# A second block's mixer in one fused kernel: where the state space tables are loaded, and in which order the SSM outputs' matmuls run

## The chip, the cores and the metric

The kernel runs on one core of a Trainium2 chip. A time is the device time of one run in microseconds; the time of a kernel is the median of its runs. All of the work is one program: TensorE (PE in the rows, its weight loads PEld) multiplies, VectorE (DVE), ScalarE (ACT) and GpSimd (POOL) do the rest, and SyncE (SP) issues nearly all transfers.

## The reference, cut to what matters

Two blocks on 256 tokens of 1024 channels. The first has four layers of attention and feed-forward; the second one hybrid layer, whose mixer is what is changed here. Half of the mixer is a state space model (SSM) of 32 groups of 16 channels with 64 states each, half is attention in 8 heads (with 256 tokens one block, so plain causal attention).

```python
h = rmsnorm(x, g_pre_mix)
z = jnp.einsum('bsd,de->bse', h, w_in)                  # 1024 -> 4 * 512
u, q, k, v = jnp.split(z, [D_SSM, D_SSM + D_ATTN, D_SSM + 2 * D_ATTN], axis=-1)
y_ssm = s5_mixer(u, ...)       # scan of the states, y = C states + d u, gelu, y * sigmoid(y w_glu + b)
y_attn = moba_attention(q, k, v)
mix = jnp.concatenate([rmsnorm(y_ssm, g_ssm_out), rmsnorm(y_attn, g_attn_out)], axis=-1)
x = x + rmsnorm(jnp.einsum('bse,ed->bsd', mix, w_out), g_post_mix)
```

## The kernel before

Tokens stand in two tiles of 128 (`t`), weights are streamed from memory once. A weight unit is 256 rows by 512 columns, 512 KB, loaded by `wload` into a buffer `raw` (4 buffers), then split into two parts, `hi` by ScalarE (line 158) and `lo` by VectorE (line 159), with 6 buffers each. `mm3` (lines 178 to 180) does three matmuls per row chunk with them. A projection of 512 columns from 1024 channels has 4 units and 48 matmuls. What is not urgent (transposes, the SSM's inflow) is put on the list `waiting`, from which `pump` emits one piece after each unit, and `drain` all.

The order of each engine's instructions is set by the tile framework at build time: an instruction goes when its data and its buffers are there by the framework's own reckoning, and of those that are ready the one that stands first in the program. Buffers belong to pools with a fixed number each: `big` has nine of 8 KB per partition, for the transposed activations (hT, a pair), the feed-forward's transposed products (fT, a pair per block), qkT, and the SSM's tables. Each engine, SyncE's queue too, then runs its list strictly in order.

The SSM works on chunks of 8 tokens. Its tables are computed from the parameters beside earlier layers and put in memory: `wd` (inflow of a chunk to the states), `ed` (decay and turn of the states, for the scan), `kd` (the response within a chunk) and `vd` (read-out of the states). `get_tables` (line 1107) fetches all of them when the mixer's norm is set up, in `mix2` (line 1388), that is before the last products of the feed-forward layer ahead. `kd` is read as overlapping windows (line 1121), two loads of 1 MB, `vd` (line 1122) too.

`mixer2` (line 1125) then runs:
- the projection to u; its rows go by small transfers (`uc`, line 1143) into chunks on partitions, are turned (`uo`, `ut`), and `inflow` (line 1171) multiplies them with `wd`. `states` (lines 1178 to 1199) scans them on VectorE into `xp`, the state before each chunk;
- one call for the projections to q and k, whose transposes go to qkT;
- the SSM outputs: two PSUM banks `yb`, of 32 x 128 tiles. A tile is in one of four quadrants of 32 partitions (`q_`) and at one of four places (`g8`) of the bank. Each takes one matmul of `ut` (128 rows) with a window of `kd`, then two of `xp` (64 rows, of the real and the imaginary part) with `vd`. `Chain` (line 252) keeps the matmuls of a bank in program order. Gelu follows per bank, into `yo`, and eight small transfers bring it back to tokens on partitions (`ys`, line 1230);
- the attention's numerators: scores (line 1244), masked maximum, exponential (line 546), transposes;
- the projection to v, the transposes of `ys`, the gate with w_glu, the weighted sums, the norms, and w_out.

Of the kernel before, what the change touches and what calls it, by code (L numbers as in the profile page):

```python
# [11 lines left out]
ALU = mybir.AluOpType  # L12
# [54 lines left out]
def tile_kernel(ctx, tc, I, out, upto=99):  # L67
# [54 lines left out]
    def load_gains(names):  # L122
        """Gains of the model's width, by channels on partitions."""
# [58 lines left out]
    def proj(xT, specs, consume, tmaj=False, kx=0, tags=(), mid=None):  # L182
        """specs: (w, first column, columns); consume(i, t, psum[:, :n]); mid: what comes after the first loads."""
# [37 lines left out]
    def outacc(acc, fT, lk, w, gk, nk, first, last, consume=None):  # L221
        """acc[t][n] += fT chunks lk.. times w's row chunks gk.. (two halves of 512 columns)."""
# [22 lines left out]
    class Chain:  # L245
        """Keeps the matmuls of one bank in program order, so that its accumulation groups stay apart."""
# [118 lines left out]
    def rope(v, nh, r2, cos, sin, tag):  # L365
        """v [128, nh, 2 * r2] in place; cos, sin [128, 2 * r2] (sin with its signs)."""
# [8 lines left out]
    def to_T2(dst, d0, src, n, t):  # L375
        """As to_T, in two parts."""
# [8 lines left out]
    def scores(o, q, k, rows, qs, ks):  # L385
        """o = q[rows, *qs].T @ k[rows, *ks], of parts."""
# [6 lines left out]
    def to_T(dst, d0, src, n, t, eng):  # L393
        """dst[:, d0 + i, tokens of t] = src[:, 128 i : 128 (i + 1)].T, i < n <= 4."""
# [14 lines left out]
    def layer_a(P, i, j, close, mid=None):  # L409
# [25 lines left out]
        def soft(hb):  # L435
            """p0 - lambda s0 / s1 p1 by heads, transposed."""
# [50 lines left out]
        # lambda  # L487
# [31 lines left out]
    def tr4(blocks, eng, aT=None):  # L519
        """Four blocks of 128 columns, transposed."""  # L520
# [12 lines left out]
    def heads(E, n, k, scale, nmx, so, p, mask=None):  # L533
        """Softmax numerators of n heads of k columns: p[:, a] = exp(scale * (E - max)), sums to so[:, a]."""
# [13 lines left out]
    def layer_b(P, i, j, close):  # L548
# [75 lines left out]
        def soft(hb):  # L624
            """Probabilities by heads, transposed."""
# [17 lines left out]
        def av(hb, oT):  # L643
            """The heads' outputs, with channels on partitions."""
# [28 lines left out]
    def layer_c(P, i, j, close):  # L673
# [13 lines left out]
        def permuted(g):  # L687
            """The tokens of a dilated group, in order of their phases."""
# [15 lines left out]
        def step(g, hb):  # L704
            """Attention of heads 8 hb .. of group g: a generator, for what is to come between its parts."""
# [25 lines left out]
            for t in range(NT):  # L731
                # keys: a group's own half of the tokens, or the band's columns
                k0 = 128 * t if g else 64 * t
                for e in range(2):
                    for pr in prs:
# [10 lines left out]
                        # statistics by head 8 hb + 2 d + e  # L746
# [34 lines left out]
        def spread(g):  # L781
            """The statistics of a dilated group, back in the order of the tokens."""
# [7 lines left out]
        def dilated(t, hb):  # L790
            """The two dilated groups in one: weighted sums in og[2], statistics in st12."""
# [7 lines left out]
        def total(t, hb, o0):  # L799
            """All groups, over the common sum, transposed."""  # L800
# [43 lines left out]
    def merge(nM, wa, wb, s, sa, sb):  # L844
        """sa, sb [128, 2, n]: (-max, sum) of two key groups; weights exp(max - common max), common sum."""
# [11 lines left out]
    def wsum(o, a, wa, b, wb):  # L857
        """o = a * wa + b * wb, by heads of 64."""
# [9 lines left out]
    class Late:  # L868
        """The vector engine, for work that others go before."""
# [13 lines left out]
    def cmul(ore, oim, ar, ai, br, bi, shape, neg=False):  # L883
        """(ore, oim) = (ar, ai) * (br, bi); neg: oim is the imaginary part's negative, of ai negated."""
# [10 lines left out]
    def ssm_tables():  # L895
        """Pieces of the work, one per step of the generator."""
# [38 lines left out]
        # angle less whole turns, the turn in three parts  # L935
# [14 lines left out]
        # (lambda - 1) / a  # L950
# [20 lines left out]
        # powers of lambda  # L971
# [9 lines left out]
        # b and c  # L981
# [22 lines left out]
        for q_ in range(2):  # L1004
            rs = slice(8 * q_, 8 * q_ + 8)
            # read-out: (re, -im) of c lambda^(i + 1)
# [5 lines left out]
            # impulse response of the first 8 steps  # L1012
# [15 lines left out]
        # the skip, at lag 0  # L1028
# [6 lines left out]
        # by half of the groups, input h, lag (7 of them negative), group of the half as (x, y), output h  # L1035
# [8 lines left out]
        # a chunk's inflow to the states: lambda^j b for the step j before its last, with (j, h) on partitions  # L1044
# [13 lines left out]
        # decay and turn of a chunk of 8 steps, and its powers  # L1058
# [21 lines left out]
    class Prep2(Prep):  # L1080
        """x becomes its rms norm of gain g1; the rest as for Prep of that, with gain g2."""
# [25 lines left out]
    def get_tables():  # L1107
        """The state space model's tables, back on chip."""
        kd, wd, vd, ed = TAB["kd"], TAB["wd"], TAB["vd"], TAB["ed"]
# [330 lines left out]
```

## Time and profile before

| | us |
|---|---|
| runs before | 1806.71, 1807.12, 1802.77 |
| median | 1806.71 |
| span of the profiled execution, first to last instruction | 1804.8 |
| median less that span | 1.9 |
| TensorE busy | 1761.0 |
| DVE busy | 1098.5 |
| ScalarE busy | 923.8 |

Times in the trace count from the first instruction of the profiled execution. A row of a timeline has start, duration, engine, line, operation, output<-inputs, shape and count; equal instructions in a row are merged, and a bracket at the end gives the idle time before and what ended it. The fp32 matmuls of the SSM and of the transposes are two instructions each in the trace; a matmul's duration there runs to its last result, so that the distance of starts, not the duration, is what one costs in a dense stretch.

### The profile page before, as it was taken

To read this page: it belongs to the slowest core of one execution; us is meant where nothing else is said; L and a number is where in the kernel's file an instruction comes from. 1 tells how busy PE (TensorE), PEld (TensorE's weight loads), DVE (VectorE), ACT (ScalarE), POOL (GpSimd) and SP (SyncE) were. 2 spreads that over 40 slices of the span, in tenths; PEclk is the share of its full clock that TensorE was granted. 3 is DMA by queue.
4 is the path that set the end of the run, shared out by engine and by line. 5 is a ranking of instruction groups with operands and counts; after the bars stand their busy time and mean duration, and the time that the engine had idled before them with its cause. 6 is when DMAs were issued, how large, how long until landed. Compare 5 with 4: busy or idle time off the path is not lost.

```text
span 1804.8 us, 24261 instructions
## 1 busy us (share of the span) xinstructions
PE 1761.0 (98%) x9008; PEld 1432.6 (79%) x9008; DVE 1098.5 (61%) x1963; ACT 923.8 (51%) x1497; POOL 71.1 (4%) x100
## 2 busy tenths in 40 slices
PE   8999999999999999999999999999999969999998
PEld 6778888878888877777878888777888857678886
DVE  6766555776554655555676655777976545475554
ACT  6655444675444565655555444674544433554443
POOL 0010000110000000000000000001000000010000
PEclk9999999999999999999999999999999989999999
DMA  7346565524666554555446565534676685346662
GB/s 257 106 124 191 184 190 177 157 94 126 189 187 188 167 141 121 150 154 162 153 118 198 183 190 186 165 117 129 192 245 208 204 211 171 100 134 204 188 187 92
DMA packets 168766, 299.56 MB, mean 166 GB/s; under 512 B 20120, under 2 KB 36464, under 8 KB 167880
## 3 DMA queue, kind: packets, MB, share of 16 engines
q1 hardware_dynamic: 164936, 293.52, 53.5%
q0 software_dynamic: 3712, 4.49, 1.0%
q8 instruction: 71, 1.16, 0.3%
q14 instruction: 47, 0.39, 0.1%
HBM read 288.20 MB, written 8.68 MB: 164 GB/s over the span
## 4 chain that ended last, share of the span: by engine, by line
PE 90%; DVE 3%; DMA 2%; ACT 2%; issue 1%; POOL 1%; SPq 0%; POOLq 0%; DVEq 0%; ACTq 0%
PE psacc L179 13%; PE psacc L180 13%; PE psacc L178 13%; PE psE L178 7%; PE psE L179 6%; PE psE L180 6%; PE psT L178 6%; PE psT L179 6%; PE psT L180 6%; PE psT L280 4%; PE psT L252 3%; PE psE L739 2%; DMA raw<-in_w_in 2%; PE psacc L252 2%; PE psE L280 1%
## 5 line engine op out<-in xcount | busy, mean ns | idle before, releaser
L159 DVE TENSOR_TENSOR lo<-raw,hi 128x1024 fp32r<-128x1024 f32 (+1 forms) x528 | 637.4, 1210 | 482.5 <-ACT hi L158 480.8
L158 ACT ACTIVATE hi<-raw 128x1024 fp32r<-128x1024 f32 (+1 forms) x528 | 552.7, 1048 | 584.5 <-PE psacc L180 239.5
L178 PE MATMUL psacc<-hi,big 128*128 128x512 f32 (+1 forms) x1136 | 456.6, 402 | 1.0 <-ACT big L272 1.0
L180 PE MATMUL psacc<-hi,big 128*128 128x512 f32 (+1 forms) x1136 | 450.1, 396 | 0.0
L179 PE MATMUL psacc<-lo,big 128*128 128x512 f32 (+1 forms) x1136 | 449.4, 396 | 0.0
L180 PEld LDWEIGHTS psacc<-hi,big 128*128 128x128 f32 x1136 | 215.0, 189 | 43.0 <-issue 0.6
L178 PEld LDWEIGHTS psacc<-hi,big 128*128 128x128 f32 x1136 | 214.8, 189 | 42.7 <-issue 2.4
L179 PEld LDWEIGHTS psacc<-lo,big 128*128 128x128 f32 x1136 | 214.7, 189 | 42.3 <-issue 1.6
L178 PE MATMUL psE<-hi,big 128*128 128x512 f32 (+2 forms) x568 | 216.0, 381 | 17.3 <-ACT hi L158 15.6
L180 PE MATMUL psE<-hi,big 128*128 128x512 f32 (+2 forms) x568 | 213.9, 377 | 0.2 <-DVE big L273 0.2
L179 PE MATMUL psE<-lo,big 128*128 128x512 f32 (+2 forms) x568 | 213.9, 377 | 0.0
L178 PE MATMUL psT<-hi,big 128*128 128x512 f32 (+1 forms) x480 | 178.5, 372 | 0.0
L180 PE MATMUL psT<-hi,big 128*128 128x512 f32 (+1 forms) x480 | 178.4, 372 | 0.0
L179 PE MATMUL psT<-lo,big 128*128 128x512 f32 (+1 forms) x480 | 178.3, 372 | 0.0
L178 PEld LDWEIGHTS psE<-hi,big 128*128 128x128 f32 x568 | 108.1, 190 | 38.1 <-ACT hi L158 16.0
L180 PEld LDWEIGHTS psE<-hi,big 128*128 128x128 f32 x568 | 107.9, 190 | 19.4 <-DVE big L273 0.9
L179 PEld LDWEIGHTS psE<-lo,big 128*128 128x128 f32 x568 | 108.2, 190 | 18.3
L178 PEld LDWEIGHTS psT<-hi,big 128*128 128x128 f32 x480 | 90.4, 188 | 15.8 <-issue 0.2
L180 PEld LDWEIGHTS psT<-hi,big 128*128 128x128 f32 x480 | 90.5, 188 | 15.7
L179 PEld LDWEIGHTS psT<-lo,big 128*128 128x128 f32 x480 | 90.5, 188 | 15.6
L546 ACT ACTIVATE p<-psE,st 128x256 f32<-128x256 f32 x96 | 44.5, 471 | 21.9 <-DVE st L544 20.0
L546 ACT ACTIVATE p<-sm,st 128x128 f32<-128x128 f32 (+2 forms) x112 | 45.9, 413 | 18.9 <-DVE st L544 18.8
(292 smaller groups left out, 1639.4 us busy)
## 6 DMA issues: line engine op xcount, KB each, us to landing
raw<-in_f_w_gu SPq DMA_DIRECT2D x176, 512.0 KB, 3.8
raw<-in_f_w_out SPq DMA_DIRECT2D x88, 512.0 KB, 3.5
raw<-in_c_w_qkv SPq DMA_DIRECT2D x72, 512.0 KB, 4.2
raw<-in_a_w_qkv SPq DMA_DIRECT2D x48, 512.0 KB, 4.2
raw<-in_w_gate SPq DMA_DIRECT2D x22, 512.0 KB, 3.7
raw<-in_w_up SPq DMA_DIRECT2D x22, 512.0 KB, 3.6
raw<-in_w_down SPq DMA_DIRECT2D x22, 512.0 KB, 3.5
raw<-in_a_w_o SPq DMA_DIRECT2D x16, 512.0 KB, 3.9
```

The source lines that it names most:

```text
L158: A.activation(hi, raw, AF.Copy)
L159: V.tensor_tensor(lo, raw, hi.bitcast(F32), op=ALU.subtract)
L178: T.matmul(o, a, hi[:, c, :n], start=(first and c == 0), stop=False)
L179: T.matmul(o, a, lo[:, c, :n], start=False, stop=False)
L180: T.matmul(o, b, hi[:, c, :n], start=False, stop=(last and c == nk - 1))
L252: ins = T.matmul(*a, **kw)
L280: T.transpose(pt[:n, i * 128:(i + 1) * 128], src, ident)
L546: A.activation(p[:, a], src[:, a], AF.Exp, bias=nmx[:, a:a + 1], scale=scale, accum_out=so[:, a:a + 1])
L739: T.matmul(E[:, k * a:k * a + k], qkT[64 * e:64 * e + 64, d, cs(t)], qkT[64 * e:64 * e + 64, 4 + d, k0:k0 + k], start=True, stop=True)
```

## The change

`get_tables` is parted in two. `get_inflow` fetches `wd` and `ed` where all tables were fetched; `get_outflow(a)` fetches the half `a` of `kd` and `vd`, and is called after the projection to q (0) and after that to k (1), which become two calls. The numerators' loop is moved ahead of the SSM outputs, with its `drain()`. The SSM outputs of a bank go by kind: first the matmuls of `ut` for all places and quadrants, then those of `xp`, by place, part and quadrant, the quadrant innermost. `start`, which clears the bank's marks in a quadrant, is set only at the first place. Comments and docstrings are dropped.

```diff
-    def get_tables():
+    def get_inflow():
-        kd, wd, vd, ed = TAB["kd"], TAB["wd"], TAB["vd"], TAB["ed"]
+        wd, ed = TAB["wd"], TAB["ed"]
         wt = [big([128, 16, 2, 64]) for _ in range(2)]
-        vt = [big([128, 16, 128]) for _ in range(2)]
-        tt_ = [big([128, 2048]) for _ in range(2)]
         rows = [work([128, 512], "sse") for _ in range(3)]
         for a in range(2):
             nc.sync.dma_start(wt[a], wd[a].rearrange("p (r g q) -> p r g q", r=16, g=2))
         for a, z in enumerate(rows):
             nc.sync.dma_start(z, ed[a])
-        for a in range(2):
-            win = kd[a, :, 0:2048]
-            nc.sync.dma_start(tt_[a], bass.AP(win.tensor, win.offset, [[256, 8], [3840, 16], [1, 2048]]))
-            nc.sync.dma_start(vt[a], vd[a].rearrange("p (r c) -> p r c", r=16))
+    def get_outflow(a):
+        kd, vd = TAB["kd"], TAB["vd"]
+        win = kd[a, :, 0:2048]
+        tt_, vt = big([128, 2048]), big([128, 16, 128])
+        nc.sync.dma_start(tt_, bass.AP(win.tensor, win.offset, [[256, 8], [3840, 16], [1, 2048]]))
+        nc.sync.dma_start(vt, vd[a].rearrange("p (r c) -> p r c", r=16))
+        return tt_, vt
...
-        proj(hT, [(w, 512, 512), (w, 1024, 512)], lambda c, t, p_: consu(1 + c, t, p_))
+        got = []
+        for c in range(2):
+            proj(hT, [(w, 512 + 512 * c, 512)], lambda _, t, p_: consu(1 + c, t, p_))
+            got.append(get_outflow(c))
+        tt_, vt = zip(*got)
...
-        yb = [psum("acc"), psum("acc")]
-        for b in range(2):
-            ym = Chain()
-            for g8 in range(4 * b, 4 * b + 4):
-                for q_ in range(4):
-                    o = yb[b][32 * q_:32 * q_ + 32, 128 * (g8 - 4 * b):128 * (g8 - 4 * b) + 128]
-                    ym(o, utv[:, g8, q_], tt_[g]...[:, pr % 4, pr // 4], start=True, stop=False)
-                    for a in range(2):
-                        ym(o, xp[a][64 * g:64 * g + 64, pr, 0:32], vt[a][64 * g:64 * g + 64, pr], start=False, stop=(a == 1))
...
         drain()
         aTs, sums = {}, {}
...
+        yb = [psum("acc"), psum("acc")]
+        for b in range(2):
+            ym, g8s = Chain(), range(4 * b, 4 * b + 4)
+            at = lambda g8, q_: yb[b][32 * q_:32 * q_ + 32, 128 * (g8 - 4 * b):128 * (g8 - 4 * b) + 128]
+            for g8 in g8s:
+                for q_ in range(4):
+                    ym(at(g8, q_), utv[:, g8, q_], tt_[g]...[:, pr % 4, pr // 4],
+                       start=(g8 == 4 * b), stop=False, skip_group_check=True)
+            for g8 in g8s:
+                for a in range(2):
+                    for q_ in range(4):
+                        ym(at(g8, q_), xp[a][64 * g:64 * g + 64, pr, 0:32], vt[a][64 * g:64 * g + 64, pr], start=False,
+                           stop=(a == 1), skip_group_check=True)
...
         proj(hT, [(w, 1536, 512)], lambda c, t, p_: consu(3, t, p_))
```

## Rows read from the trace of the kernel before

**Rows 1.** The page's first part: busy time, share of the span, instructions

```profile
PE 1761.0 (98%) x9008; PEld 1432.6 (79%) x9008; DVE 1098.5 (61%) x1963; ACT 923.8 (51%) x1497; POOL 71.1 (4%) x100
```

**Rows 2.** The chain of waits in order of time, 1430 to 1620: start, us, what

```profile
1449.62 31.54 DMA raw<-in_w_in
...
1521.36 26.94 PE psacc L252 x184
```

**Rows 3.** Stretches: length, then busy time (count) per engine, clock, DMA share, GB/s

```profile
1437.00:1461.70 24.70, 24.70 (x119) 20.01 (x118) 14.76 (x22) 11.67 (x19) 1.10 (x2) 1.00 0.97 251
...
1466.70:1482.35 15.65, 0.07 (x1) 0.00 (x1) 0.02 (x1) 1.11 (x2) 0.00 (x0) 0.59 0.70 158
1482.35:1486.73 4.38, 4.38 (x11) 3.47 (x11) 3.94 (x7) 3.86 (x8) 1.46 (x1) 0.51 0.57 203
...
1519.02:1548.23 29.21, 29.21 (x200) 15.95 (x199) 8.37 (x10) 4.68 (x7) 0.00 (x0) 1.00 0.34 109
1548.23:1569.40 21.17, 21.17 (x107) 15.07 (x107) 13.81 (x51) 15.97 (x44) 0.00 (x0) 1.00 0.45 119
```

**Rows 4.** TensorE's waits, 1470 to 1610: total us, times, longest

```profile
PE psE L178 <- ACT hi L158: 15.6, 1, 15.6
```

**Rows 5.** SyncE's queue in order of time

```profile
1348.13 2.69 SPq L1056 DMA_DIRECT2D wd<-sswt  x4
...
1437.21 0.37 SPq L155 DMA_DIRECT2D raw<-in_w_in  x1
1437.75 1.29 SPq L1117 DMA_DIRECT2D sse<-ed  x3
...
1440.36 0.97 SPq L1115 DMA_DIRECT2D big<-wd  x2
1441.42 0.69 SPq L1121 DMA_DIRECT2D big<-kd  x1
...
1449.62 38.64 SPq L155 DMA_DIRECT2D raw<-in_w_in  x7
```

**Rows 6.** Stretches of 5 us, columns as in rows 3

```profile
1445.00:1450.00 5.00, 5.00 (x24) 4.14 (x23) 2.64 (x3) 1.70 (x3) 0.00 (x0) 1.00 1.06 383
1450.00:1455.00 5.00, 5.00 (x26) 3.97 (x25) 3.21 (x4) 1.30 (x4) 0.00 (x0) 1.00 1.01 156
```

**Rows 7.** TensorE in order of time, within the SSM outputs

```profile
1523.39 0.41 PE L252 MATMUL psacc<-big,ut 128*32 128x128 f32 x2
1523.73 0.62 PE L252 MATMUL psacc<-big,xp 64*32 64x128 f32 x4
1524.28 0.41 PE L252 MATMUL psacc<-big,ut 128*32 128x128 f32 x2
```

**Rows 8.** TensorE where parts of its array alternate: layers a, b, the tables (line 252)

```profile
45.62 0.29 PE L389 MATMUL psE<-big,big 64*128 64x256 f32 x2
45.74 0.29 PE L390 MATMUL psE<-big,big 64*128 64x256 f32 x2
...
375.18 2.00 PE L252 MATMUL psT<-big,big 128*64 128x256 f32 x16
...
1278.30:1279.81 1.51, 1.51 (x63) 1.51 (x64) 1.00 0.91 283
```

**Rows 9.** From the SSM outputs' end to `ys`: timeline, and transfers' us to landing

```profile
1548.23 0.55 PE L280 MATMUL psT<-con,qs 128*128 128x128 f32 x3
...
1552.41 0.69 DVE L1227 SCALAR_TENSOR_TENSOR yo<-ga,yh 128x512 f32<-128x512 f32 x1
...
1553.24 5.13 SPq L1230 DMA_DIRECT2D ys<-yo  x8
...
ys<-yo SPq DMA_DIRECT2D x8, 64.0 KB, 2.4
```

**Rows 10.** Timeline: the last part of u scaled, the last step of the states

```profile
1491.49 0.69 ACT L1139 ACTIVATE qs<-psE,r 128x512 f32<-128x512 f32 x1 [0.18 <-PE psE L180]
...
1519.22 0.68 DVE L1132 TENSOR_TENSOR xp<-xp,z 128x512 f32<-128x512 f32 x1
```

More of the change, by code (lines that the diff above doesn't have):

```diff
@@ L1117, in get_tables @@
             nc.sync.dma_start(z, ed[a])
-        for a in range(2):
-            win = kd[a, :, 0:2048]
-            nc.sync.dma_start(tt_[a], bass.AP(win.tensor, win.offset, [[256, 8], [3840, 16], [1, 2048]]))
-            nc.sync.dma_start(vt[a], vd[a].rearrange("p (r c) -> p r c", r=16))
-        TAB["got"] = wt, vt, tt_, rows
+        TAB["in"] = wt, rows
+    def get_outflow(a):
[5 more added lines that the diff above has]
+        return tt_, vt
     def mixer2(P, close):
         hT, r = P.hT, P.r
-        wt, vt, tt_, (e_, i_, d_) = TAB["got"]
+        wt, (e_, i_, d_) = TAB["in"]
         w = I["w_in_2"][0]
@@ L1203, in mixer2 @@
         nc.sync.dma_start(caus, I["consts"][:, o_:o_ + w_].rearrange("p (t k) -> p t k", t=NT))
-        proj(hT, [(w, 512, 512), (w, 1024, 512)], lambda c, t, p_: consu(1 + c, t, p_))
-        yb = [psum("acc"), psum("acc")]
-        yo = work([128, 8, 8, 16], "yo")
-        ys = work([128, NT, 512], "ys")
-        for b in range(2):
-            ym = Chain()
-            for g8 in range(4 * b, 4 * b + 4):
-                for q_ in range(4):
-                    g, pr = q_ // 2, (q_ % 2) * 8 + g8
-                    o = yb[b][32 * q_:32 * q_ + 32, 128 * (g8 - 4 * b):128 * (g8 - 4 * b) + 128]
-                    ym(o, utv[:, g8, q_], tt_[g].rearrange("p (i x y h) -> p x y i h", x=4, y=4, h=16)[:, pr % 4, pr // 4],
-                       start=True, stop=False)
-                    for a in range(2):
-                        ym(o, xp[a][64 * g:64 * g + 64, pr, 0:32], vt[a][64 * g:64 * g + 64, pr], start=False, stop=(a == 1))
-            yh = work([128, 8, 64], "yh")
-            A.activation(yh.rearrange("p i (g h) -> p g i h", g=4), yb[b].rearrange("p (g i h) -> p g i h", g=4, i=8), AF.Copy, scale=0.5)
-            ga = work([128, 8, 64], "ga")
-            A.activation(ga, yh, AF.Square, scale=2.0)
-            V.tensor_scalar(ga, ga, 0.044715, 1.0, op0=ALU.mult, op1=ALU.add)
-            tt(ga, ga, yh, ALU.mult)
-            A.activation(ga, ga, AF.Tanh, scale=2.0 * math.sqrt(2.0 / math.pi))
-            V.scalar_tensor_tensor(yo[:, :, 4 * b:4 * b + 4].rearrange("p i g h -> p i (g h)"), ga, 1.0, yh, op0=ALU.add, op1=ALU.mult)
-        for t in range(NT):
-            for q_ in range(4):
-                nc.sync.dma_start(ys[:, t, cs(q_)], yo[32 * q_ + 16 * t:32 * q_ + 16 * t + 16].rearrange("c i g h -> c i (g h)"))
+        got = []
[3 more added lines that the diff above has]
+        tt_, vt = zip(*got)
         drain()
@@ L1249, in mixer2 @@
                     aTs[t, e, pr] = tr4([p_[:, a, cs(c)] for a in range(n) for c in range(t + 1)], (A, V)[e])
+        yb = [psum("acc"), psum("acc")]
+        yo = work([128, 8, 8, 16], "yo")
+        ys = work([128, NT, 512], "ys")
+        for b in range(2):
[3 more added lines that the diff above has]
+                for q_ in range(4):
+                    g, pr = q_ // 2, (q_ % 2) * 8 + g8
+                    ym(at(g8, q_), utv[:, g8, q_], tt_[g].rearrange("p (i x y h) -> p x y i h", x=4, y=4, h=16)[:, pr % 4, pr // 4],
+                       start=(g8 == 4 * b), stop=False, skip_group_check=True)
+            for g8 in g8s:
+                for a in range(2):
+                    for q_ in range(4):
+                        g, pr = q_ // 2, (q_ % 2) * 8 + g8
+                        ym(at(g8, q_), xp[a][64 * g:64 * g + 64, pr, 0:32], vt[a][64 * g:64 * g + 64, pr], start=False,
+                           stop=(a == 1), skip_group_check=True)
+            yh = work([128, 8, 64], "yh")
+            A.activation(yh.rearrange("p i (g h) -> p g i h", g=4), yb[b].rearrange("p (g i h) -> p g i h", g=4, i=8), AF.Copy, scale=0.5)
+            ga = work([128, 8, 64], "ga")
+            A.activation(ga, yh, AF.Square, scale=2.0)
+            V.tensor_scalar(ga, ga, 0.044715, 1.0, op0=ALU.mult, op1=ALU.add)
+            tt(ga, ga, yh, ALU.mult)
+            A.activation(ga, ga, AF.Tanh, scale=2.0 * math.sqrt(2.0 / math.pi))
+            V.scalar_tensor_tensor(yo[:, :, 4 * b:4 * b + 4].rearrange("p i g h -> p i (g h)"), ga, 1.0, yh, op0=ALU.add, op1=ALU.mult)
+        for t in range(NT):
+            for q_ in range(4):
+                nc.sync.dma_start(ys[:, t, cs(q_)], yo[32 * q_ + 16 * t:32 * q_ + 16 * t + 16].rearrange("c i g h -> c i (g h)"))
         proj(hT, [(w, 1536, 512)], lambda c, t, p_: consu(3, t, p_))
@@ L1391, in mix2 @@
         nxt = Prep2(I["final_norm"], gains("final_norm"), gains("g_pre_mix_2"))
-        get_tables()
+        get_inflow()
         return nxt
```

## The prediction, made before the changed kernel was run

> **What bounds the kernel now.** TensorE is busy 98% of the span [rows 1], so a gain has to come out of its idle time or make its work shorter; other engines matter only where TensorE waits for them. I read the chain of waits next, for the second block's mixer. Two pieces of it are long [rows 2]: one load of w_in that is 31.54 us from issue to landing, and 184 instructions of line 252, the SSM outputs, in one run of 26.94 us. The table of stretches gives their weight [rows 3]: after 1466.70 TensorE does nothing for 15.65 us, then runs 11 instructions in 4.38 us at a granted clock of 0.51, the lower of its two levels (1.2 GHz); the SSM outputs fill 29.21 us; from there to 1569.40 the numerators and the v projection take 21.17 us. The list of waits names the idle time: the matmul waits 15.6 us for ScalarE's part `hi` of a weight [rows 4]. SyncE's queue says why [rows 5]: between the second and the third unit of w_in stand `ed`, `wd` and the four loads of `kd` and `vd`, 4 MB that nobody reads before the SSM outputs, and the third unit, issued at 1449.62, lies behind them. The queues stay full, but from 1450 on the rate falls from 383 to 156 GB/s [rows 6]: these tables are slow to read. The first two units, 24 matmuls, keep TensorE busy only to 1466.70.
>
> **Part 1, the loads.** `get_inflow` keeps `wd` and `ed` where they were; `get_outflow(0)` comes after the q projection in the program, `get_outflow(1)` after k. Nothing is added: the same 4 MB in the same four issues. With the third and fourth unit of w_in no longer behind them, they should land before 1461.7, when TensorE comes to them. Removed are the wait, 15.6 us, and the slow clock behind it: 11 instructions at the 0.21 us of the stretch before (24.70 us for 119) are 2.3 us, so 4.38 - 2.3 = 2.1 us. Sum 17.7 us, at most; below nothing this edit alone can't go, since u then has only fewer bytes ahead of it.
>
> What it triggers is the price. The queue's order isn't the program's: the framework sends a load when its buffer is free. The first unit of w_in went ahead of `ed` [rows 5], which the program has earlier. So the tables' place is set by the buffers `big`, nine in all, which I take to be granted in the order of first use: the new hT pair, written just before u's first matmuls, comes before the first `kd` and `vd`, and qkT before the second. The first pair then goes out near 1460. 2.1 MB at 156 GB/s are 13.4 us, to 1473. Queued behind it are the last units of q, the first of k, and the small transfers `uc`, which start the chain to the states; SyncE's queue is in order, and ScalarE, which converts weights in order, holds the scaling of u behind a late unit. u's 48 matmuls last to 1461.8 + 48 x 0.21 = 1472 and two more units lie ready, 5 us, so the cover is just enough. The states end 28 us after u does, as now (the last part of u is scaled at 1491.49, `xp` is done at 1519.9 [rows 10]), so near 1502 to 1506, when k also ends. The second pair can't go before qkT's turn, near 1490, and lands near 1505: the SSM outputs may wait a few us for it. I take 2 us for this part's stalls, with ends 0 and 17: the upper end is two pairs of 13.4 us, each with only two units (5 us) of cover.
>
> **Part 2, the order of the SSM outputs' matmuls.** Each fp32 matmul is two instructions, so 96 matmuls are 192 instructions, before and after. Now each tile of y takes one matmul of `ut` (128 rows by 32 columns) and two of `xp` (64 rows by 32) before the next. Three rows price it [rows 7]: two instructions of `ut` take 0.34 us from start to start, four of `xp` 0.55. Two more cost 0.21, so one costs 0.105 and each change of the array's shape 0.34 - 0.21 = 0.13 us. Check: 192 x 0.105 + 64 x 0.13 = 28.5 us; the stretch of 29.21 us holds 200 instructions [rows 3], eight of them transposes of about 0.1 us each, which leaves 28.3. By kind, the 64 changes become about four, 0.5 us: without anything else 20.7 us.
>
> Quadrants in turn should do more. Where column parts of the array alternate, the trace shows them at work at once [rows 8]: layer b's 16 instructions of 256 columns on two halves take 2.00 us, 0.125 each, where 256 columns in a row would take 2 x 0.105 = 0.21, a factor of 1.7; the tables' own 64 instructions on four quadrants, half of 16 columns and half of 112, take 1.51 us (63 are recorded), where 64 x 0.105 x 64/128 = 3.4 us would be due, a factor of 2.2. In this kernel today a quadrant never gets the next one beside it, since a change of shape stands between. Four full-width quadrants lie between 2.2 and 1.7 squared, 2.9; I take 2.6: 20.2 / 2.6 + 0.5 = 8 us. Gain 28.3 - 8 = 20.3 us, ends 7.6 (no overlap) and 21.
>
> The `xp` matmuls use two row halves as well, 0 to 63 for quadrants 0 and 1 and the rest for 2 and 3, all into one bank. The only rows with both halves at work are layer a's scores: two pairs of 256 columns start 0.12 us apart [rows 8], into two banks. The Trainium skill, TensorEngine Tiling (Array Packing), "Gotcha 1: PSUM Pressure", says that different row tiles can't access the same bank at once; no row here shows that case. By that rule the `xp` part would overlap by halves only, which is the third rival below.
>
> **Part 3, numerators ahead.** The scores, softmax and transposes move ahead of the SSM outputs, with no instruction more. Their work is DVE's and ScalarE's; in the 21.17 us of that stretch ScalarE is busy 15.97 and DVE 13.81 [rows 3], beside TensorE's v projection. Now the SSM outputs can stand beside it too. What is behind the SSM outputs instead is their own chain: from TensorE's last instruction (1548.23) where the transposes of `qs` follow, through gelu to `yo` (1552.41 + 0.69) 4.9 us, eight issues of `ys` 5.13, landing 2.4: 12.4 us until `ys` can be transposed [rows 9]. The v projection, 48 x 0.21 = 10.1 us, still lies behind them as cover, and 2.4 us show, 0 if numerators' transposes fill them, 12.4 if v was used up as filler before. `drain()` now also brings the last transposes of k before the scores, which had stood at 1548 behind the SSM outputs; that is 0.5 us, moved. I take 2 us.
>
> **The sum**, against the profiled execution (1804.8 us of span, 1.9 below the median of 1806.71): 17.7 + 20.3 - 2 - 2 = 34. Span 1770.8, median 1772.7, so 1773.
>
> **The rivals.**
> - No overlap of quadrants: the instructions accumulate into one bank and go one by one. The SSM outputs take 20.7 instead of 8 us: 1773 + 12.7 = 1786. For it: no row has 128-column streams on four quadrants. Against: both groups in rows 8 accumulate in one bank too.
> - Tables in the weights' way: the 13.4 us of each pair show but for 5, 17 us instead of 2: 1788. For it: 31.54 us behind two pairs [rows 2]; q, k and v ask for 0.5 MB each 2.5 us, 200 GB/s, more than the 156 left. Against: u covers the first pair, and v isn't needed until the SSM outputs are.
> - Row halves exclude each other in a bank: `ut` 64 x 0.105 / 2.6 = 2.6, `xp` 128 x 0.105 / 1.7 = 7.9, changes 0.5: 11 us, 3 more: 1776. It is the page's rule named above; as mechanism, two halves of the array would have to wait for each other at PSUM. Neither for nor against it is there a row.
> - The change doesn't do what it says: if buffers are granted as they come free and not by first use, `kd` and `vd` go out at 1441 as before, ahead of the third unit. The front's 17.7 us stay, its 2 us of stalls don't come: 1773 + 15.7 = 1789. For it: loads did overtake each other [rows 5]. Against: `wd` was written by 1351, yet read only at 1440.36 [rows 5]. In between the feed-forward layer held hT and at most two pairs of fT, six of the nine buffers, so some were free; that fits grants in order, in which the last fT pair comes first.
> - Slower: both pairs stand right ahead of units that TensorE needs at once, and each unit lands after 31.5 us, as the one in rows 2 did; with 5 us of cover, 26 us show twice. 1806.7 - 17.7 - 20.3 + 52 = 1821. It decides from where the two waits together pass 38 us, 24 us per landing. Against: that landing stood behind two pairs, not one.
>
> **How the numbers follow.** Forecast 0.60, no overlap 0.06, tables in the way 0.13, row halves 0.08, no move 0.08, slower 0.05. The forecast's own range is 1764 (no stalls, factor 2.9, some 5 us better, and scatter) to 1781. With the rivals up to 1789 the range is 1763 to 1790; it leaves out the last case and tails. A measurement of this kernel tells about 0.3%, 5.4 us, from no change: faster 0.93 (all but the last, less a little), same 0.02, slower 0.05.
>
> **What would show it.** Right: no wait of over 3 us of the w_in matmuls for `hi`, and full clock from 1461 to the SSM outputs; `kd` issued after the third and fourth unit; line 252's 192 instructions within 8 us, starts of different quadrants closer than 0.1 us; k ending near 1504 and `ys` transposed near 1534 on the trace's clock. Wrong: a wait for `raw` in q or k of 8 us or more (tables in the way); 20 us for line 252 (no overlap); 7 to 8 us for the `xp` part (row halves); the 15.6 us still there (no move); a wait of TensorE for `big` ahead of the first SSM output, which would say that the second pair came late. Outside this mixer nothing should move.

## The result, and the profile after

The changed kernel takes 1782.74 us (median of four runs, 1781.37 to 1797.92) against 1805.13 before: a ratio over all runs of 0.9899, 95% interval 0.9876 to 0.9923 (the quotient of the medians is 0.9876). Forecast were 1773 and a range of 1763 to 1790. Executions of this kernel differ by the clock that TensorE is granted, so a mean clock stands beside a time where it matters: the profiled one is the longest (span 1796.1, mean clock 0.984), the three others have 0.993. A second set of four runs, on another chip, gave 1775.83 to 1791.23 (ratio 0.9871, 0.9833 to 0.9908).

TensorE's waits from 1430 to 1610 in the changed kernel's profile, in the columns of [rows 4] (total us, times, longest), the longest three:

```profile
PE psT L280 <- DMA ys<-yo: 5.0, 1, 5.0
PE psacc L252 <- DMA big<-kd: 3.6, 1, 3.6
PE psT L280 <- ACT qs L1142: 1.8, 1, 1.8
```

The wait of 15.6 us for `hi` [rows 4] is gone. New are a wait for the tables ahead of the SSM outputs and one for `ys` behind them. SyncE's queue, as in [rows 5]:

```profile
1444.28 9.47 SPq L155 DMA_DIRECT2D raw<-in_w_in  x4
1453.87 0.69 SPq L1124 DMA_DIRECT2D big<-kd  x1
...
1463.71 8.10 SPq L155 DMA_DIRECT2D raw<-in_w_in  x4
1471.86 9.66 SPq L1146 DMA_DIRECT2D uc<-qs  x6
...
1482.25 9.22 SPq L155 DMA_DIRECT2D raw<-in_w_in  x6
1491.56 0.67 SPq L1124 DMA_DIRECT2D big<-kd  x1
```

`kd` goes out behind the last two units of u and the first two of q, the second pair behind k's and even v's units. The chain of waits has that second load as one piece of 18.47 us:

```profile
1491.56 18.47 DMA big<-kd
```

Stretches of the changed kernel, columns as in [rows 3] (length, busy us and count of each engine, clock, DMA share, GB/s): the SSM outputs and numerators, v, the wait for `ys`, what follows.

```profile
1509.50:1539.50 30.00, 29.43 (x198) 15.81 (x198) 9.25 (x42) 9.51 (x29) 0.00 (x0) 0.50 0.20 73
1540.00:1553.50 13.50, 13.50 (x97) 10.59 (x96) 8.60 (x13) 8.81 (x18) 1.86 (x1) 1.00 0.52 162
1553.50:1558.50 5.00, 0.04 (x1) 0.00 (x0) 1.50 (x2) 2.21 (x3) 0.00 (x0) 0.81 0.71 203
1558.50:1563.60 5.10, 4.59 (x15) 3.46 (x16) 1.03 (x2) 1.19 (x2) 0.00 (x0) 0.52 0.75 186
```

In this execution TensorE ran 30 us at 1.2 GHz, busy for 29.43 of them; at 2.4 GHz that work is worth about half. The other runs, 14 to 17 us shorter, fit a stretch without it, and the first experiment shows one.

For all kernels one measure is used below: the **stage**, from u's first matmul (line 178 into `psE`) to the first weighted sum (`psE<-vs,aT`), which takes in what the change moves. Its ends are starts in each kernel's timeline; the time is the median of its runs, its ratio goes against before's runs on the same chip. What follows the stage takes 228.4 to 228.5 us in every trace. What stands ahead of it does not stay the same: the stage starts between 1456.1 and 1463.9, with a mean clock from 700 to 900 us of 1.00 in e3 and e7 and 0.96 in the first profile and e11. So two times can differ by up to 8 us that have nothing to do with the change, and the stage is the safer measure. The ratios leave out executions over 1.5% above the fastest of their kernel; these are five of e2's ten, all of them among its seven at a lower clock, so that its ratio mixes both groups and differs from its median.

| kernel | stage, us | time, us | ratio (interval) |
|---|---|---|---|
| before | 1461.80 to 1576.45: 114.65 | 1805.13 | |
| changed, first profile | 1463.35 to 1567.64: 104.29 | 1782.74 | 0.9899 (0.9876 to 0.9923) |
| e1, changed, again | 1458.15 to 1550.42: 92.27 | 1780.03 | 0.9871 (0.9833 to 0.9908) |
| e2, loads alone | 1462.49 to 1561.79: 99.30 | 1813.08 | 0.9967 (0.9926 to 1.0009) |
| e3, matmul order alone | 1456.21 to 1549.82: 93.61 | 1787.38 | 0.9893 (0.9867 to 0.992) |
| e4, numerators back behind | 1463.03 to 1542.10: 79.07 | 1769.65 | 0.9802 (0.9781 to 0.9823) |
| e5, e4 without quadrants in turn | 1460.76 to 1553.37: 92.61 | 1780.68 | 0.986 (0.9839 to 0.9882) |
| e6, numerators ahead alone | 1459.51 to 1581.89: 122.38 | 1812.1 | 1.0034 (1.0018 to 1.005) |
| e7, changed, second pair early | 1456.12 to 1547.10: 90.98 | 1782.56 | 0.9867 (0.9846 to 0.9887) |
| e8, e4, second pair early | 1458.96 to 1550.91: 91.95 | 1781.31 | 0.986 (0.9838 to 0.9881) |
| e9, changed, kd behind k | 1460.82 to 1555.57: 94.75 | 1783.87 | 0.9886 (0.9864 to 0.9908) |
| e10, e4, kd behind k | 1463.01 to 1551.42: 88.41 | 1779.85 | 0.9857 (0.9833 to 0.988) |
| e11, e4 again | 1463.93 to 1546.95: 83.02 | 1771.7 | 0.9821 (0.9798 to 0.9844) |
| e12, e4, kd behind the chunks of u | 1461.69 to 1543.59: 81.90 | 1771.84 | 0.9821 (0.9802 to 0.9839) |

### The profile page after: what moved, and what is told of

It is laid out like the page before. It is cut to its first block, busy times and chain, and to the rows that moved or that the text cites. A ratio compares the mean times of both kernels' runs of the same rounds, so it can differ in the third digit from the quotient of the medians.

```text
span 1796.1 us, 24258 instructions
## 1 busy us (share of the span) xinstructions
PE 1756.4 (98%) x9008; PEld 1428.5 (80%) x9008; DVE 1099.8 (61%) x1963; ACT 924.5 (51%) x1497; POOL 76.9 (4%) x100
## 4 chain that ended last, share of the span: by engine, by line
PE 89%; DVE 4%; DMA 3%; ACT 2%; issue 1%; POOL 1%; SPq 0%; POOLq 0%; DVEq 0%; ACTq 0%
PE psacc L179 13%; PE psacc L180 13%; PE psacc L178 13%; PE psE L178 6%; PE psE L180 6%; PE psE L179 6%; PE psT L178 6%; PE psT L179 6%; PE psT L180 6%; PE psT L280 5%; PE psT L252 3%; PE psE L739 2%; PE psE L280 1%; DVE lo L159 1%; DMA big<-kd 1%
## 5 line engine op out<-in xcount | busy, mean ns | idle before, releaser
L180 PEld LDWEIGHTS psT<-hi,big 128*128 128x128 f32 x480 | 90.4, 188 | 15.7
L179 PEld LDWEIGHTS psT<-lo,big 128*128 128x128 f32 x480 | 90.4, 188 | 15.6
L546 ACT ACTIVATE p<-sm,st 128x128 f32<-128x128 f32 (+2 forms) x112 | 45.9, 413 | 20.7 <-DVE st L544 20.7
```

What stands on the lines that cost most here:

```text
L179: T.matmul(o, a, lo[:, c, :n], start=False, stop=False)
L180: T.matmul(o, b, hi[:, c, :n], start=False, stop=(last and c == nk - 1))
L546: A.activation(p[:, a], src[:, a], AF.Exp, bias=nmx[:, a:a + 1], scale=scale, accum_out=so[:, a:a + 1])
```

## The experiments

### The changed kernel once more: what varies

> The changed kernel itself, once more, for a second profile. In its profiled execution (span 1796.1 us) TensorE's granted clock was 0.50 from about 1509 to 1539 us, while the three timed runs took 1781 to 1783 us. Theory: these runs kept the full clock there. Then a profile with a span near 1780 us shows a clock of 1.00 in that stretch, the stretch is about 15 us shorter, and the two waits before it (1.8 us for the scaled q/k, 3.6 us for kd) are shorter or gone. Rival: the low clock stands there in every run and the 15 us lie elsewhere; then a profile near 1780 us shows 0.50 there too and is shorter at the front or behind the mixer.

Its profile (span 1778.8) has the full clock where the first had the half. The same stretches:

```profile
1506.00:1524.10 18.10, 18.10 (x238) 11.05 (x235) 8.96 (x41) 10.65 (x33) 0.00 (x0) 1.00 0.27 97
1524.10:1536.40 12.30, 12.30 (x60) 9.55 (x56) 8.93 (x15) 7.67 (x15) 2.05 (x1) 1.00 0.55 180
1536.40:1541.20 4.80, 0.03 (x1) 0.06 (x1) 1.46 (x2) 2.21 (x3) 0.00 (x0) 0.82 0.72 206
1541.20:1546.30 5.10, 4.63 (x15) 3.42 (x16) 1.10 (x2) 1.19 (x2) 0.00 (x0) 0.50 0.77 175
```

The stage is 12.0 us shorter. The waits ahead of it are hardly so: 2.4 us for `qs`, 1.6 for `kd`, against 1.8 and 3.6. So the theory holds for the place, and the waits alone don't settle when the clock falls. Of the 17.3 us between the two spans the other 5.2 lie ahead of the stage. One profile can be an unlucky one: the first misses the median by 15 us.

### The loads alone

Before, with `get_inflow` and `get_outflow` as in the change, and the rest as it was:

```diff
-        proj(hT, [(w, 512, 512), (w, 1024, 512)], lambda c, t, p_: consu(1 + c, t, p_))
+        got = []
+        for c in range(2):
+            proj(hT, [(w, 512 + 512 * c, 512)], lambda _, t, p_: consu(1 + c, t, p_))
+            got.append(get_outflow(c))
+        tt_, vt = zip(*got)
```

> Before with part 1 alone: the tables' loads parted and moved, the SSM outputs tile by tile and the numerators behind them as before. Theory (loads worth 17.7 us at the front, less 1.8 and 3.6 us of waits that the changed kernel's trace shows ahead of the SSM outputs): 1805 - 12 = 1793 us. If those waits bring the clock down as in the changed kernel's profile, the SSM outputs' 28 us run at half the clock and the time is 1807 to 1821 us. Rival: the tables only move the wait, and all 17.7 us come back at q, k or the SSM outputs: 1805 us with the clock up.

In the profile, at full clock, the stage is 15.35 us shorter; TensorE waits 0.9 us for `vd` and nothing for `kd` or `qs`. The runs fall in two groups: three of 1787 to 1793 us (mean clock 0.994 to 0.999), seven of 1812 to 1815 (0.981 to 0.983). The long ones have no trace. By the clock alone, 0.0125 of 1800 us lost at half speed is 1800 x 0.0125 / 0.5 = 45 us at 1.2 GHz and so 22 us more, which is the distance of the groups. In the execution with a trace the loads do what was predicted. That the long ones lose it in this mixer is not shown. Over all ten runs the loads alone gain nothing that can be measured, and seven of the ten are 7 to 10 us slower than before.

### The order of the matmuls alone

Before, with the SSM outputs by kind and quadrants in turn:

```diff
             for g8 in range(4 * b, 4 * b + 4):
                 for q_ in range(4):
                     ym(o, utv[:, g8, q_], ..., start=True, stop=False)
-                    for a in range(2):
-                        ym(o, xp[a][64 * g:64 * g + 64, pr, 0:32], ...)
+            for g8 in g8s:
+                for a in range(2):
+                    for q_ in range(4):
+                        ym(at(g8, q_), xp[a][64 * g:64 * g + 64, pr, 0:32], ...)
```

> Before with part 2 alone: the SSM outputs by kind, quadrants in turn; loads and numerators where they were. Theory: at full clock an instruction costs 0.031 us (40 of them in 1.23 us in the changed kernel's trace) against 0.147 on average before, 192 x 0.031 = 6 us plus changes of kind, 28.3 - 6.5 = 22 us gained: 1783 us, since numerators and the v projection follow as before and cover the way to ys. Rival: the work that follows (gelu, softmax on DVE and ScalarE) was partly covered by the long SSM outputs, and TensorE waits for it: 1790 us or more. Rival without overlap (predicted 20.7 us for the outputs): 1797 us.

The groups of TensorE's instructions by form from 1509 to 1521 (busy us, mean ns | idle before):

```profile
L252 PE MATMUL psacc<-big,xp 64*32 64x128 f32 x128 | 4.1, 271 | 0.0
L252 PE MATMUL psacc<-big,ut 128*32 128x128 f32 x64 | 2.6, 276 | 0.0
```

The durations add up to 4.1 + 2.6 = 6.7 us. By the distance of starts, the measure by which before's are 28.3, they are 3.9 + 2.3 = 6.2 us: a gain of 22 us, and the stage is 21.0 us shorter. A wait of 1.8 us for the copies of k's transposes, which now have no long stretch beside them, takes some of it. The median, 1787, lies between the theory (1783) and the rival (1790); the profiled run took 1780 at a mean clock of 0.996, the others 1787 to 1789 at 0.989 to 0.992. The stage of the profiled run starts 5.6 us earlier than before's.

### The numerators back behind the SSM outputs

The changed kernel, with the block of the numerators moved back, behind the loop that issues `ys`:

```diff
-        drain()
-        aTs, sums = {}, {}
...
         yb = [psum("acc"), psum("acc")]
...
                 nc.sync.dma_start(ys[:, t, cs(q_)], ...)
+        drain()
+        aTs, sums = {}, {}
...
```

> The changed kernel with part 3 undone: SSM outputs ahead of the numerators, loads and order of matmuls as changed. Theory: the wait for ys (5.0 us, and the rest of a chain of 7.6 us with the slow restart behind it) goes, since the numerators and v stand behind the SSM outputs again: 1782 - 7 = 1775 us. Rival: softmax of the numerators then has no cover, and the time is 1782 to 1786 us.

The stage is 35.6 us shorter than before, and 13.2 than in e1. The theory's 7 us are about half of that. `ys` is late by nothing. The end of the chain in its timeline (start, duration), where no wait stands at the transposes:

```profile
1518.78 0.69 DVE L1241 SCALAR_TENSOR_TENSOR yo<-ga,yh 128x512 f32<-128x512 f32 x1
...
1519.60 5.15 SPq L1244 DMA_DIRECT2D ys<-yo  x8
...
1535.04 1.04 PE L280 MATMUL psT<-con,ys 128*128 128x128 f32 x8
```

The last SSM output ends at 1514.2, so the chain to the last issue of `ys` takes 10.6 us, and ten more pass before TensorE comes to the transposes. This is the version that beats both kernels: 1769.65 us against 1780.03 of the changed kernel on the same chip.

### Quadrants not in turn

e4 with the loops over places inside the loop over quadrants:

```diff
-            for g8 in g8s:
-                for a in range(2):
-                    for q_ in range(4):
+            for q_ in range(4):
+                for g8 in g8s:
+                    for a in range(2):
```

(and likewise for the matmuls of `ut`).

> The kernel of e4 (SSM outputs ahead of the numerators), with one thing changed: within a kind the quadrant is the outermost loop, so that consecutive matmuls stay in one quadrant; the number of changes of kind is as in e4, up to the six more that the quadrants' row halves bring. Theory (quadrants in turn overlap, 0.031 us per instruction against 0.105 in one quadrant): 192 x (0.105 - 0.031) = 14 us longer, 1769.7 + 14 = 1784 us. Rival (the gain came from the 64 changes of shape alone, and an instruction costs 0.031 us in any order): 1770 to 1771 us.

Its timeline within the SSM outputs, where the clock is full, and the groups by form from 1504 to 1528:

```profile
1514.79 10.87 PE L252 MATMUL psacc<-big,xp 64*32 64x128 f32 x124
```

```profile
L252 PE MATMUL psacc<-big,xp 64*32 64x128 f32 x128 | 11.9, 273 | 0.0
```

124 instructions in about 10.8 us are 0.087 us each, where e3 has 128 in 3.9 by the distance of starts, 0.030 each: one quadrant after the other costs 2.9 times as much, though the changes of kind are as few. It is 11 us more in the median and 13.5 in the stage, of which 2.3 are a longer wait for `kd` (3.4 against 1.1 us); behind it the clock is 0.50 from 1506 to 1511, which e4's is not. The rival of the changes of shape alone falls. But they pay too: by the distance of starts, line 252 takes 28.3 us before, 19.5 here (some of it at the lower clock) and 6.5 in e4. So about 9 us of part 2's gain are the changes of shape, where 7.6 were predicted, and at most 13 the quadrants in turn.

### The numerators ahead alone

Before, with the block of the numerators in front of the SSM outputs:

```diff
+        drain()
+        aTs, sums = {}, {}
...
         yb = [psum("acc"), psum("acc")]
...
         # causal attention: numerators
-        drain()
-        aTs, sums = {}, {}
...
```

> Before with part 3 alone: the numerators ahead of the SSM outputs, loads and matmul order as before. Theory (behind the SSM outputs only v's 48 matmuls, 10.9 us, cover a way to ys that is 12.4 us or, behind the softmax and the weights' halves in ScalarE's and DVE's queues, 16 us): 3 to 8 us longer, 1808 to 1813 us. Rival (the numerators' DVE and ScalarE work now lies beside the SSM outputs and their stretch gets shorter): 1797 to 1803 us.

1812.1 against 1805.44 us: part 3 by itself makes the kernel 6.7 us slower, as the theory had it, and the stage 7.7 us longer. The wait is of the same kind as in the changed kernel:

```profile
PE psT L280 <- DMA ys<-yo: 4.4, 2, 4.1
```

### Where the second pair can go

Four kernels ask for the second pair elsewhere. In e7 and e8 the call is made after k's first unit, for the changed kernel and for e4:

```diff
+            if c:
+                waiting.insert(0, lambda: got.append(get_outflow(1)))
             proj(hT, [(w, 512 + 512 * c, 512)], lambda _, t, p_: consu(1 + c, t, p_))
-            got.append(get_outflow(c))
+            if c == 0:
+                got.append(get_outflow(0))
```

> The changed kernel, with the second pair of kd and vd asked for after the first unit of k instead of behind all of k: kd then goes out behind the first pair, vd ahead of k's weights. Theory (the waits of 1.6 to 3.6 us for kd and of 2 us for the scaled q/k ahead of the SSM outputs bring the clock down in some executions, which is why they spread from 1776 to 1798 us): without those waits the clock stays up, and the runs lie within 5 us of each other, near 1774 to 1777 us. Rival (the clock falls without them too): the same spread. Rival (three loads in a row stand ahead of q's last units): TensorE waits 5 us or more in q, 1785 us.

> The kernel of e4 with the second pair asked for as in e7. Theory: the remaining wait for kd (1.1 us) goes, 1768 to 1769 us. Rival: kd's place ahead of q's last units and vd's ahead of k's costs more than that, 1772 us or more.

SyncE's queue in e7, and TensorE's two longest waits there:

```profile
1448.24 0.63 SPq L1124 DMA_DIRECT2D big<-kd  x1
1456.49 5.59 SPq L155 DMA_DIRECT2D raw<-in_w_in  x3
1464.31 19.99 SPq L1146 DMA_DIRECT2D uc<-qs  x6
```

```profile
PE psacc L178 <- ACT hi L158: 5.7, 1, 5.7
PE psT L280 <- DVE uo L1159: 2.0, 1, 2.0
```

Asked for ahead of qkT's first use, the table gets its buffer at once and goes out right behind the first pair, 36 us earlier, counted from u's first matmul, than in the changed kernel: it was the buffer that held it, in the order of first use. The wait then stands in q (5.7 us; 3.1 in e8), and the chunks of u (`uo`) are late. Runs of e7 lie between 1777 and 1784 us: a narrower spread, but no gain. The wait in q is the one that its second rival named. e8 is slower than e4, by 0.6% of before, which was its rival. Its profile has the clock at the lower level again, among the numerators this time, behind a wait of 2.4 us for the copies of k's transposes:

```profile
1521.00:1526.00 5.00, 5.00 (x12) 2.83 (x10) 1.81 (x14) 3.70 (x13) 0.00 (x0) 0.50 0.49 81
```

e9 and e10 part the pair: its `vd` ahead, behind the first pair, its `kd` late by priority, behind k's last unit.

```diff
+                def later():
+                    with tc.high_priority(-60):
+                        got.append(get_outflow(1))
+                waiting.insert(0, later)
...
+        if a:
+            vt = big([128, 16, 128])
+            nc.sync.dma_start(vt, vd[a].rearrange("p (r c) -> p r c", r=16))
+        tt_ = big([128, 2048])
         nc.sync.dma_start(tt_, ...)
```

> The changed kernel, numerators ahead, with the second pair parted: its vd, quick to read, right behind the first pair, its kd, slow to read, behind k's last weight unit and ahead of v's four units (before: behind them). Theory (the waits of 1.6 to 3.6 us for kd and 2 us for the scaled q/k bring the clock down in some executions, and it comes back late among the small matmuls): kd is then there when k ends, TensorE waits for it 0 to 0.5 us, the clock stays up, and the runs lie within 5 us of each other, near 1774 us; the wait for ys, 5 us, stays. Rival: the spread of 1776 to 1798 us stays without that wait.

> The kernel of e4 (SSM outputs first) with the loads of e9. Theory: the wait for kd (1.1 us in e4's trace) goes and nothing takes its place: 1767 to 1769 us, no run above 1773 us. Rival: vd ahead of q's third unit costs its 1 MB, 2.7 us at 383 GB/s, in q: 1771 to 1772 us.

TensorE doesn't wait for `kd` any more, and waits longer for other things, in e9:

```profile
PE psT L280 <- ACT qs L1145: 7.9, 1, 7.9
PE psT L280 <- DVE uo L1162: 3.2, 1, 3.2
```

Both theories fall: e9 1784 and e10 1780 us, and e10's rival (1772) too. Both waits have one form in e9's chain of waits. Behind three tables in a row a unit of w_in, issued at 1466.41, takes 12.01 us to land; ScalarE has its conversion ahead of the scaling of u's last part, so that the small transfers of u are late and their six issues take 13.00 us (8.18 in e11, 10.10 in e4). Behind `kd` another, issued at 1489.77, takes 16.22 us; ScalarE stands 8.70 us for it, ahead of the scaling of q. e10 has the same, 16.39 and 9.39 us for the second. e4 once more, beside them:

> The kernel of e4 once more, on the chip of e9 and e10. Theory: 0.980 of before again, 1769 to 1771 us, with now and then a run 5 to 15 us longer, where the wait for kd has brought the clock down. Rival: e4's four runs, within 3 us of each other, are the rule, and none is longer.

1771.7 us, four runs of 1767 to 1777, the longest at the lowest mean clock (0.992 against 0.995 to 0.997). Its profile has a wait for `kd` of 4.9 us.

The last kernel holds the second pair back until the chunks of u are there, and takes its buffers ahead of qkT's:

```diff
+        if behind is not None:
+            for z in (tt_[0:1, 0:1], vt[0:1, 0, 0:1]):
+                G.tensor_copy(z, behind[0:1, 7, 7, 0:1])
```

> The kernel of e4, with kd and vd of the second pair held back by nothing but the chunks of u: a one-element copy out of them into each table's buffer, by GpSimd, stands ahead of its load, and the buffers are taken ahead of qkT's. In SyncE's queue the pair then stands behind the small transfers of u and k's last unit, and ahead of v's four units (in e4: behind those, 8 us later). Theory (the wait for kd, 1.1 and 4.9 us in the traces of e4 and e11, is those 8 us, and e10 lost because its early loads held up the small transfers, not for another reason): no wait for kd, nor for the chunks or the scaled q/k; 1766 to 1768 us, all runs within 4 us. Rival: the pair now lies beside k's last units and v's, and one of these is late by as much: 1770 us or more, as e4 and e11.

The pair now goes out at 1481.51, ahead of v's units. No wait for `kd`, none for the chunks, and 4.5 us for the scaled q. The chain of waits, and ScalarE's timeline:

```profile
1482.76 18.80 DMA raw<-in_w_in
```

```profile
1501.65 1.06 ACT L158 ACTIVATE hi<-raw 128x1024 fp32r<-128x1024 f32 x1 [6.12 <-DMA raw<-in_w_in]
1502.61 0.67 ACT L1145 ACTIVATE qs<-psacc,r 128x512 f32<-128x512 f32 x1
```

A unit of w_in right behind the pair takes 18.80 us to land. TensorE doesn't need it yet, but ScalarE's queue has its conversion ahead of the scaling of q, and stands for 6.12 us, as in e9 and e10. So the rival holds, and the theory's account of e10 falls: 1771.84 us, the ratio of e11, with runs within 2.2 us of each other. Where `kd` was put ahead of units of w_in, these came late, and the order of ScalarE's queue brought that to TensorE. Behind v's units, as in the change, is as good as any place that was tried.

## Why the prediction was right and where it was wrong

**The sum.** A gain of 34 us was forecast, and 22.4 were measured (25.4 in e1). The forecast's own range ended at 1781, and the median, 1782.74, lies beyond it. It falls into the stated range because that was widened for rivals, none of which came about as a whole: that is luck. (e1's median, 1780.03, is inside both.) Most of what is missing lies in part 3, as follows.

**The loads (part 1) came as predicted, where the clock stayed up.** Predicted: 17.7 us less 2 of stalls, 15.7; measured in e2's stage 15.35, in one execution at full clock. (`ed` stood between the first two units of w_in before, not behind the second as the prediction has it, which changes nothing in the sum.) That this edit alone can't make the kernel slower was wrong: seven of e2's ten runs are slower than before. The framework does grant the buffers in the order of first use (e7), the first pair left at 1453.87 (predicted near 1460), the second at 1491.56 (near 1490), whose `kd` was there 18.5 us later, 5 us after the time that was predicted. k ends at 1505.7 (predicted 1504), and the wait of TensorE for the tables, named as the sign of a late second pair, came: 3.6 us in the first profile, 1.1 to 4.9 in those of e1, e4 and e11.

**The order of the matmuls (part 2) was somewhat better than predicted.** 8 us were forecast for the SSM outputs, with an overlap of 2.6; e3 shows 6.2 by the distance of starts, and the gain of 22 us lies just beyond the upper end of 21. The factor between e5 and e3 is 2.9, the upper value that was considered. The two rivals that lived on this step fall with it: without overlap (20.7 us), and with row halves that exclude each other (11 us). The Trainium skill, TensorEngine Tiling (Array Packing), "Gotcha 1: PSUM Pressure", says that different row tiles can't access one bank at once. In e3's trace no such effect shows: the `xp` instructions, which change the row half after every second quadrant while they write one bank, cost 3.9 / 128 = 0.030 us each, the `ut` instructions with all rows 2.3 / 64 = 0.037.

**Parts 1 and 2 together** were forecast at 17.7 - 2 + 20.3 = 36.0 us; e4, which is these two, has a stage shorter by 35.6 and a median shorter by 35.7. That they agree so closely is in part chance: part 2 gave more than was forecast, and waits of 1.8 and 1.1 us took it back.

**The numerators ahead (part 3) is the step that failed.** It was taken at 2 us, with ends of 0 and 12.4; it costs 10.4 in the medians (1780.03 in e1, 1769.65 in e4) and 13.2 in the stage of the change, 6.7 and 7.7 by itself (e6). The term was made of a chain of 12.4 us less a cover of 10.1. The cover was no shorter: v, with some transposes, runs from 1524.1 to 1536.4 in e1. The chain was not. It was read where nothing stood in its way, and in e1 it reads:

```profile
1522.86 1.30 PE L252 MATMUL psacc<-big,xp 64*32 64x128 f32 x40
...
1527.38 0.57 ACT L1253 ACTIVATE yh<-psacc 128x512 f32<-128x512 f32 x1
...
1533.72 1.06 ACT L158 ACTIVATE hi<-raw 128x1024 fp32r<-128x1024 f32 x1 [1.66 <-PE psacc L180]
1534.68 0.61 ACT L1258 ACTIVATE ga<-ga 128x512 f32<-128x512 f32 x1
...
1535.95 0.68 DVE L1259 SCALAR_TENSOR_TENSOR yo<-ga,yh 128x512 f32<-128x512 f32 x1
...
1536.71 5.18 SPq L1262 DMA_DIRECT2D ys<-yo  x8
...
1541.17 1.30 PE L280 MATMUL psT<-con,ys 128*128 128x128 f32 x5 [4.77 <-DMA ys<-yo]
```

From the last SSM output (1524.1) to the last `yo` (1536.6) it is 12.5 us instead of 4.9: the first gelu step waits behind the numerators' exponentials, the last behind `hi` of a w_out unit that itself waits for TensorE to free a buffer. That makes 17.1 us to the transposes. Three things show: the 4.8 us of waiting; a lower clock behind it (0.50 for 5.1 us, 4.63 of them busy, so 2.3 us); and the SSM outputs, which the framework mixed with scores and transposes, mostly in pieces of six or eight. A part of its timeline, and their groups in e1, beside those of e3 above:

```profile
1512.93 0.42 PE L252 MATMUL psacc<-big,xp 64*32 64x128 f32 x8
1513.28 0.33 PE L280 MATMUL psT<-con,p 128*128 128x128 f32 x1
1513.54 0.42 PE L252 MATMUL psacc<-big,xp 64*32 64x128 f32 x8
```

```profile
L252 PE MATMUL psacc<-big,xp 64*32 64x128 f32 x128 | 6.5, 277 | 0.0
...
L252 PE MATMUL psacc<-big,ut 128*32 128x128 f32 x64 | 3.6, 281 | 1.6 <-DMA big<-kd 1.6
```

The durations add up to 10.1 us instead of 6.7; by the distance of starts it is 8.9, against 6.5 in e4. So part 3 undoes a piece of part 2, 2.4 us, a coupling that the prediction didn't look at. 4.8 + 2.3 + 2.4 = 9.5 us of the 13.2 between the stages of e1 and e4 are explained by this. Another 2.7 lie ahead of the SSM outputs: 1.1 us more of waits (2.4 and 1.6 against 1.8 and 1.1), and eight matmuls at 0.43 us instead of 0.23, at the lower clock behind the first wait. Whether part 3 brings these isn't shown, and 1 us stays open. The medians differ by less, 10.4, also because the front ahead of the stage differs between executions. That the order of a block also decides what the framework mixes into it was open to see: it takes of the ready instructions the first in the program, and the scores were ready.

The price is not one of the order alone. The kernels with the second pair moved come in twins too, and there part 3 costs 1.3 us in the medians (e7 against e8) and 4.0 (e9 against e10; 6.3 in the stage). TensorE's waits for `ys` with the numerators ahead, in e7 and in e9, and the first transposes of `ys` in e7:

```profile
PE psT L280 <- DMA ys<-yo: 0.9, 3, 0.4
```

```profile
PE psT L280 <- DMA ys<-yo: 1.1, 4, 0.4
```

```profile
1538.61 0.49 PE L280 MATMUL psT<-con,ys 128*128 128x128 f32 x3
```

In e7 the last SSM output ends at 1526.7, so the way to the transposes is 11.9 us, about the 12.4 that were predicted, and v covers nearly all of it. There ScalarE's last step of gelu runs for both banks together, where two conversions of weights part them in e1, and the last `yo` is done 8.1 us behind the last SSM output. So the cover was rightly judged; what was missed is that the framework may put other work into the chain's queues, which it did in e1 and e6, and not in e7 and e9.

**The clock was in no term.** The prediction gave back the 2.1 us behind the old wait and asked nothing of the new ones. Short waits ahead of a long stretch of small matmuls cost more than their length when the clock falls there: 12 us of the stage between the two profiles of one kernel, whose waits ahead of the SSM outputs differ by 1.4 us. The other 5.2 us between these two lie ahead of the stage, where the clock varies too. So it is the clock, more than the length of the stalls, that parts the two executions with a trace; for the other runs this isn't shown. What decides whether it falls isn't settled: in e1 it was 0.75 from 1496 to 1501 and 0.91 from 1501 to 1506, and then full for the stretch.

**The other rivals and signs.** Tables in the weights' way: in part, a few us, as above. No move: refuted by the queue. Slower: refuted for the whole, though part 3 alone is slower. Of the signs for being right two failed: line 252 within 8 us (8.9 in e1, more in the first profile) and `ys` transposed near 1534 (1541.2 and 1558.5).

## What to carry to other kernels

When work is moved ahead of a chain, price the chain with that work in the queues of the engines it runs through; a duration read where nothing stood in its way can be too short. Small matmuls that fill different quadrants of the array pay most in one unbroken run, so look at what the scheduler will mix into them. And take more than one profile of a kernel whose runs differ by more than the effect that is studied, and compare the part of the trace that the change touches.

## What the runs showed of the hardware

- Four quadrants of 32 columns with 128 columns to stream, into one bank, overlap by a factor of 2.9: 0.030 us per `xp` instruction in turn, 0.087 in one quadrant (e3, e5).
- The granted clock stayed at its lower level for 30 us while TensorE was busy for 29.43 of them, with 32-column and 64-row matmuls, transposes and fp32 scores; before, it rose after 11 full matmuls in 4.38 us [rows 3].
- Behind the reads of `kd` the DMA engines are about half idle: while TensorE stands still and waits for the unit of w_in behind the tables, the DMA share of e3 is 0.50 (same columns as above)

```profile
1471.00:1476.00 5.00, 0.00 (x0) 0.00 (x0) 0.00 (x0) 0.69 (x1) 0.00 (x0) 0.50 0.50 194
```

The Trainium skill, DMA: Bandwidth & Descriptors, "Why a DMA increments its semaphore by 16 and not by 1", says that a load is spread over the largest number of engines, up to 16, that divides the slowest dimension on either side; the windows of `kd` have 8 there. The share fits it, but no view here shows which engines were at work. Loads with 16 as the slowest dimension were not tried.
